# Solving the delta rule's triangular systems in the first stage, pair by pair and group by group

## The chip, the cores and the metric

The kernel runs on one core of a Trainium2 chip. The metric is the device time of one execution in microseconds (us). A core has five engines with instruction queues of their own: TensorE (PE, with its weight loads as PEld), VectorE (DVE), ScalarE (ACT), GpSimd (POOL) and SyncE (SP), which here issues nearly all DMA transfers. Each engine takes its instructions in order; they wait for each other through semaphores. PE multiplies into PSUM banks, and another engine has to copy a bank out before it can be used again.

## The reference

One layer of a hybrid block on 1024 tokens with 16 learned meta tokens ahead of them (L = 1040), 1024 channels, float32:

```python
proj = rms_norm(h) @ w_in                 # attention q, k, v, forget logits; recurrent inputs rw; gates
rw_prev = rw shifted by one token
z = rw + mu * (rw_prev - rw)              # r, k, v and the low-rank inputs zw, za, zg
w = w0 + tanh(zw) @ w_up ; a = sigmoid(a0 + za @ a_up) ; g = sigmoid(zg) @ g_up
# recurrent branch, 8 heads of 64:  S_t = S_(t-1) diag(w_t) + (S_(t-1) a_t) b_t^T + v_t k_t^T ; y_t = S_t r_t
o_rwkv = (group_norm(y) + bonus) * g
o_fox  = forgetting attention of 8 heads of 64
merged = sigmoid(gates) * (o_fox @ w_bf, o_rwkv @ w_br)
h = h + merged @ w_o ; out = h + conv_ffn(rms_norm(h))
```

## The kernel before

All large products are exact to about float32: operands are split into a high and a low part of type fp32r, and `mm3` makes three products of each (lines L201, L202, L203; tiles `mm`, `gate`, `dn`, `aux`). Weights come in pieces of 128x512 (`wf`), from which ACT makes `wh` and POOL `wl`.

Stage 0 normalises the input. Stage 1 prepares the recurrent branch, head pair by head pair (four pairs, p = 0 to 3, of 128 channels): three projections (`zk`, `zr`, `zv`, each in three pieces of 346 or 348 columns by `rw_tile`), the low-rank products (`aux`, L304 to L312, into `sw`, `tha`, `g`), a running sum along the tokens (`cs`, L319), its exponentials `ex` and `ei`, the norm of the keys (`ss`, `inv` with Ln and Exp on ACT and a Newton step on DVE), and from these the tiles `ar_t` and `bk_t` of 17 chunks of 64 tokens. All DVE operations of this kind take the 1088 tokens of a pair in one instruction. `prods` multiplies bk and ar of a chunk (L394) and masks the result into `am` (L395), which goes to the array `am_d` in DRAM. `diags` copies the 32x32 diagonal blocks of `am_d` to a second array `a_d` (L404, four DMAs a pair). `bkt` transposes bk (L411) and stores it through `bt` (L414, L415). `bonus` and transposed values are stored as well. The gate projections serve as filler, and the last of their 84 stage-1 steps are emitted behind pair 3.

Stage 2 begins with `forget` (L582), then merges two streams by hand-set costs: the attention, and the recurrent branch. The latter first solves the triangular systems of two chunks at a time (`rw_pre`, b = 0 to 8): their blocks are loaded from `a_d` to 128 lanes (`la`), a unit matrix to `x`, and 31 steps of a multiplication and an addition on DVE (L449 and L451) invert them. The result goes to `t_d` in DRAM and from there into the diagonal blocks of `am`; 16 products of 32x32 a chunk on PE (`rp`, L474 and L478) give the off-diagonal block. `rw_chain` then takes the 17 chunks one behind the other (`ch`). Stage 3 joins the branches, stages 4 and 5 are the output projection and the convolutional feed-forward.

The text of the program does not fix the order on an engine alone: a scheduler with a model of the chip orders the instructions of each engine when the kernel is built. PSUM has three banks for `mm`, two for `aux`, two shared by `am` and `tp`, and one for `gate` in stage 1.

Of the kernel before, what the change touches and what calls it, by code (L numbers as in the profile page):

```python
# [100 lines left out]
def stage0(S, p0):  # L101
    nc, tc = S.nc, S.tc
# [7 lines left out]

    def tiles(*tags):
        r = []
        for t in tags:
            m = 6 if t[1:] in ("r_t", "k_t") else 3
            r.append(p0.tile([P, m, 348], F32, name="xt", tag=t))
        return r, [(i, j) for i, t in enumerate(r) for j in range(t.shape[1])][:KD]

    xs = []
    for c, (t0, t1) in enumerate(CH):
        n = t1 - t0  # L120
        tl, at = tiles(*(("zr", "zv", "sw"), ("tha", "inv", "ex"), ("ar_t", "cs"))[c])
        k = 0
        for t in tl:
            for j in range(0, t.shape[1], 3):
                m = min(3, KD - k)
                nc.sync.dma_start(out=t[:, j:j + m, :n], in_=S.A["xT"][:, k:k + m, t0:t1])
                k += m
                if k == KD:
                    break
        xs.append([tl[i][:, j] for i, j in at])  # L130
# [1066 lines left out]
```

## Time and profile before

| | us |
|---|---|
| median of 3 runs | 2045.58 (2042.92 to 2048.2) |
| the profiled execution's span | 2045.7 |
| PE busy | 1879.8 (92%) |
| DVE busy | 918.6 (45%) |
| ACT busy | 751.7 (37%) |
| POOL busy | 558.8 (27%) |

The span of the profiled execution is the whole program, so its own time is the span. In the profile each instruction has a start and a duration; a group of instructions with one source line and tile has a minimum, median and maximum duration in ns. A table of stretches gives each engine's busy time in the stretch, the number of its records in brackets (a plain float32 matmul leaves two), the clock granted to PE (PEclk, 1.00 is full speed), the share of the DMA engines and GB/s. The matmuls' records overlap, so the cost of one in a row of them is the distance of their starts. A row of the waits reads "engine, line <- what it waited for: us in total, times, the longest".

### The profile page before, as it was taken

To read this page: it belongs to the slowest core of one execution; us is meant where nothing else is said; L and a number is where in the kernel's file an instruction comes from. 1 tells how busy PE (TensorE), PEld (TensorE's weight loads), DVE (VectorE), ACT (ScalarE), POOL (GpSimd) and SP (SyncE) were. 2 spreads that over 40 slices of the span, in tenths; PEclk is the share of its full clock that TensorE was granted. 3 is DMA by queue.
4 is the path that set the end of the run, shared out by engine and by line. 5 is a ranking of instruction groups with operands and counts; after the bars stand their busy time and mean duration, and the time that the engine had idled before them with its cause. 6 is when DMAs were issued, how large, how long until landed. Compare 5 with 4: busy or idle time off the path is not lost.

```text
span 2045.7 us, 32875 instructions
## 1 busy us (share of the span) xinstructions
PE 1879.8 (92%) x12812; PEld 1699.0 (83%) x12812; DVE 918.6 (45%) x2032; ACT 751.7 (37%) x1603; POOL 558.8 (27%) x552
## 2 busy tenths in 40 slices
PE   7996966747899999999899999999999999999999
PEld 6985855646778888888778999899998998999997
DVE  5264534128678642432764545733232332332333
ACT  5542332214333443443665434532232331322321
POOL 6421111103102211311431234533232332332322
PEclk9997979868999899999999999999999999999999
DMA  4233232541334332222223533211111111111112
GB/s 153 79 104 92 93 95 84 163 109 52 87 109 116 105 95 85 83 65 61 73 87 123 146 120 112 79 42 57 47 42 52 41 53 42 42 57 47 42 48 102
DMA packets 154483, 167.95 MB, mean 82 GB/s; under 512 B 47576, under 2 KB 111112, under 8 KB 154328
## 3 DMA queue, kind: packets, MB, share of 16 engines
q1 hardware_dynamic: 154072, 165.79, 27.0%
q8 instruction: 101, 1.65, 0.3%
q14 instruction: 54, 0.44, 0.1%
q0 software_dynamic: 256, 0.07, 0.0%
HBM read 123.39 MB, written 43.53 MB: 82 GB/s over the span
## 4 chain that ended last, share of the span: by engine, by line
PE 78%; DVE 7%; DMA 6%; SPq 4%; ACT 2%; issue 1%; POOL 0%; ACTq 0%; DVEq 0%; POOLq 0%
PE mm L202 14%; PE mm L201 14%; PE mm L203 14%; PE dn L201 4%; PE dn L203 4%; PE dn L202 4%; SPq L404 3%; PE gate L201 3%; PE gate L202 2%; PE gate L203 2%; PE t L780 2%; PE o L794 2%; PE am L394 2%; DVE x L451 1%; DVE xt L449 1%
## 5 line engine op out<-in xcount | busy, mean ns | idle before, releaser
L189 POOL TENSOR_TENSOR wl<-wf,wh 128x512 fp32r<-128x512 f32 (+1 forms) x268 | 352.6, 1319 | 787.3 <-ACT wh L188 738.2
L202 PE MATMUL mm<-x,wh 128*128 128x344 f32 (+1 forms) x1056 | 339.1, 321 | 0.0
L201 PE MATMUL mm<-x,wh 128*128 128x344 f32 (+1 forms) x1056 | 337.6, 320 | 1.1 <-DVE ug L1029 1.0
L203 PE MATMUL mm<-x,wl 128*128 128x344 f32 (+1 forms) x1056 | 337.4, 320 | 1.0 <-POOL wl L189 1.0
L188 ACT CAST wh<-wf 128x512 fp32r<-128x512 f32 (+1 forms) x268 | 163.7, 612 | 352.6 <-PE dn L202 182.4
L201 PE MATMUL mm<-xh,wh 128*128 128x348 f32 (+4 forms) x624 | 211.8, 341 | 3.6 <-ACT xh L169 1.6
L202 PE MATMUL mm<-xl,wh 128*128 128x348 f32 (+4 forms) x624 | 210.2, 337 | 0.7 <-POOL xl L170 0.7
L203 PE MATMUL mm<-xh,wl 128*128 128x348 f32 (+4 forms) x624 | 209.5, 336 | 0.0
L201 PEld LDWEIGHTS mm<-x,wh 128*128 128x128 f32 x1056 | 199.2, 189 | 1.9 <-ACT uv L1027 1.2
L203 PEld LDWEIGHTS mm<-x,wl 128*128 128x128 f32 x1056 | 199.0, 189 | 1.7 <-POOL wl L189 1.5
L202 PEld LDWEIGHTS mm<-x,wh 128*128 128x128 f32 x1056 | 199.3, 189 | 0.4
L201 PE MATMUL gate<-xh,wh 128*128 128x342 f32 x384 | 142.8, 372 | 2.9 <-ACT sg L834 2.9
L1056 DVE TENSOR_TENSOR h<-h,dn 128x512 f32<-128x512 f32 x96 | 66.0, 689 | 169.0 <-PE dn L203 168.4
L203 PE MATMUL dn<-gh,wl 128*128 128x512 f32 x352 | 138.8, 394 | 0.0
L201 PE MATMUL dn<-gh,wh 128*128 128x512 f32 x352 | 138.6, 394 | 0.0
L202 PE MATMUL dn<-gl,wh 128*128 128x512 f32 x352 | 138.6, 394 | 0.0
L201 PEld LDWEIGHTS mm<-xh,wh 128*128 128x128 f32 x624 | 121.9, 196 | 9.1 <-issue 4.1
L202 PEld LDWEIGHTS mm<-xl,wh 128*128 128x128 f32 x624 | 122.0, 196 | 5.9 <-issue 1.5
L202 PE MATMUL gate<-xl,wh 128*128 128x342 f32 x384 | 126.6, 330 | 0.0
L203 PE MATMUL gate<-xh,wl 128*128 128x342 f32 x384 | 126.2, 329 | 0.0
L203 PEld LDWEIGHTS mm<-xh,wl 128*128 128x128 f32 x624 | 121.8, 195 | 3.7 <-issue 1.0
L1028 DVE SCALAR_TENSOR_TENSOR uv<-mm,par,uv 128x342 f32<-128x342 f32 (+1 forms) x66 | 37.8, 573 | 162.4 <-ACT uv L1027 162.4
(313 smaller groups left out, 3704.2 us busy)
## 6 DMA issues: line engine op xcount, KB each, us to landing
wf<-in_w_up_dram SPq DMA_DIRECT2D x88, 256.0 KB
am<-am_d SPq DMA_DIRECT2D x17, 512.0 KB
sg_d<-sg SPq DMA_DIRECT2D x48, 171.0 KB
sg<-sg_d SPq DMA_DIRECT2D x48, 171.0 KB
wf<-in_w_gate_dram SPq DMA_DIRECT2D x32, 256.0 KB
wf<-in_w_out_dram SPq DMA_DIRECT2D x32, 256.0 KB
wf<-in_w_down_dram SPq DMA_DIRECT2D x32, 256.0 KB
wf<-in_w_rw_dram SPq DMA_DIRECT2D x28, 256.0 KB
```

Of the source, the lines that this page charges most:

```text
L188: nc.scalar.copy(out=wh[:, :n], in_=wf[:, :n])
L189: nc.gpsimd.tensor_tensor(out=wl[:, :n], in0=wf[:, :n], in1=wh[:, :n], op=ALU.subtract)
L201: nc.tensor.matmul(ps, lhsT=wh, rhs=xh, start=first and k == 0, stop=False)
L202: nc.tensor.matmul(ps, lhsT=wh, rhs=xl, start=False, stop=False)
L203: ins = nc.tensor.matmul(ps, lhsT=wl, rhs=xh, start=False, stop=last and k == n - 1)
L394: nc.tensor.matmul(ps[:, j * P:(j + 1) * P], lhsT=bk_t[r, c0 + j, :], rhs=ar_t[r, c0 + j, :], start=True, stop=True)
L404: nc.sync.dma_start(out=S.a_d[:, k, h], in_=S.am_d[:, r, h, r])
L449: nc.vector.tensor_tensor(out=tv, in0=x[:, :ni, s:s + 1].broadcast_to([P, ni, m]), in1=la[:, s:s + 1, s + 1:s + 1 + m].broadcast_to([P, ni ...
L780: S.last_pe = nc.tensor.transpose(ps[:r, (2 * j + e) * 116:(2 * j + e) * 116 + nq], pb[e][i][:nq, k:k + r], S.ident[:nq, :nq])
L794: S.last_pe = nc.tensor.matmul(po[64 * e:64 * e + 64, :nq], lhsT=vt[:r, kb, 64 * e:64 * e + 64], rhs=pt[:r, 2 * j + e, :nq], start=kb == 0 ...
L1028: nc.vector.scalar_tensor_tensor(out=t[:, :n], in0=ps[:, 1:1 + n], scalar=cw(1), in1=t[:, :n], op0=ALU.mult, op1=ALU.add)
L1056: nc.vector.tensor_tensor(out=hs, in0=hs, in1=ps[:], op=ALU.add)
```

## The change

Stage 1 now goes by pair and group of tokens (`G`: 384, 384 and 272 tokens). What was a tile of 1088 tokens is a small tile of 390 columns, all of them drawn from one pool of 28 places (`U`, tag "u"); `ar` and `bk` have six chunks and two places each. The low-rank products take their operands unsplit, one float32 product each in place of three. After the three units of a pair, `solve` inverts that pair's systems on chip: POOL copies the upper left 64x64 of each `am` to `at`; 64 products with the unit matrix bring the 32x32 blocks of 34 chunk-heads and two diagonal places to 98 lanes (`x`); 60 DVE operations invert them; 64 products bring them back, and 64 more make the off-diagonal blocks; one DMA stores `at` as `t_d[p]`. Gone are `a_d`, `la`, the loads of `x` and the stores and loads of `t_d` by parts, and the whole of `rw_pre`. In stage 2 `rw_am` loads `am` and the inverse `tt` for each chunk, and the chain starts at once.

```diff
-CH = [(0, 346), (346, 692), (692, 1040)]
+G = [(0, 384), (384, 768), (768, 1040)]
+NU = 28
...
+def solve(S, p1, p, at):
+    nc = S.nc
+    n = 2 * NCH
+    x = p1.tile([P, 32, 32], F32, name="x", bufs=1)
+    nc.gpsimd.memset(x[32:64], 0.0)
+    for f in range(2):
+        ps = psum(S, "am")
+        for t in range(16):
+            for k in range(2):
+                nc.tensor.matmul(ps[64 * k:64 * k + n, 32 * t:32 * t + 32], lhsT=at[:, :, 32 * k + 16 * f + t],
+                                 rhs=S.ident[0:64, 32 * k:32 * k + 32], start=True, stop=True)
+        for k in range(2):
+            r = slice(64 * k, 64 * k + n)
+            nc.scalar.copy(out=x[r, :, 16 * f:16 * f + 16], in_=ps[r].rearrange("p (t s) -> p s t", s=32))
+    nl = 64 + n
+    nc.gpsimd.memset(x[:nl].rearrange("p s t -> p (s t)")[:, 0:1024:33], 1.0)
+    tmp = p1.tile([P, 240], F32, name="xm", bufs=1)
+    for s in range(1, 31):
+        m = 31 - s
+        tv = tmp[:nl, :s * m].rearrange("p (i t) -> p i t", i=s)
+        nc.vector.tensor_tensor(out=tv, in0=x[:nl, :s, s:s + 1].broadcast_to([nl, s, m]),
+                                in1=x[:nl, s:s + 1, s + 1:].broadcast_to([nl, s, m]), op=ALU.mult)
+        nc.vector.tensor_tensor(out=x[:nl, :s, s + 1:], in0=x[:nl, :s, s + 1:], in1=tv, op=ALU.add)
+    for i, (t0, nt) in enumerate(((0, 11), (11, 11), (22, 10))):
+        ps = psum(S, "am")
+        for t in range(nt):
+            for k in range(2):
+                nc.tensor.matmul(ps[32 * k:32 * k + 32, n * t:n * t + n], lhsT=x[:nl, :, t0 + t],
+                                 rhs=S.ident[:nl, 64 * k:64 * k + n], start=True, stop=True)
+        for k in range(2):
+            r = slice(32 * k, 32 * k + 32)
+            cp = nc.scalar.copy if (i + k) % 2 else nc.vector.tensor_copy
+            cp(out=at[r, :, 32 * k + t0:32 * k + t0 + nt], in_=ps[r, :n * nt].rearrange("p (t c) -> p c t", c=n))
+    hs = p1.tile([64, n, 32], F32, name="hs", bufs=1)
+    nc.vector.transpose(out=hs[0:32], in_=at[0:32, :, 0:32])
+    for f in range(2):
+        ps = psum(S, "am")
+        pv = ps.rearrange("p (h t) -> p h t", t=32)
+        for j in range(16):
+            nc.tensor.matmul(pv[32:64, j], lhsT=at[0:32, 16 * f + j, 32:64], rhs=hs[0:32, 16 * f + j], start=True, stop=True,
+                             tile_position=(0, 32))
+        nc.scalar.copy(out=hs[32:64, 16 * f:16 * f + 16], in_=pv[32:64])
+    for f in range(2):
+        ps = psum(S, "am")
+        pv = ps.rearrange("p (h t) -> p h t", t=32)
+        for j in range(16):
+            nc.tensor.matmul(pv[0:32, j], lhsT=hs[32:64, 16 * f + j], rhs=at[32:64, 16 * f + j, 32:64], start=True, stop=True,
+                             tile_position=(32, 0))
+        nc.scalar.copy(out=at[0:32, 16 * f:16 * f + 16, 32:64], in_=pv[0:32])
+    nc.sync.dma_start(out=S.t_d[p], in_=at[:])
...
+        U = lambda name: p1.tile([P, 390], F32, name=name, tag="u", bufs=NU)
...
+        def proj(p, i):
+            w = wload(S, S.A["w_rw"][2 + 3 * p + i], KD)
+            z = []
+            for c, (t0, t1) in enumerate(G):
+                z.append(U(("zk", "zr", "zv")[i]))
+                rw_tile(S, p1, 2 + 3 * p + i, z[c][:, :t1 - t0], w, c)
+            pads(z[2])
+            return z
...
+        def lora(p, c):
+            pc = slice(p * P, (p + 1) * P)
+            t0, t1 = G[c]
+            n = t1 - t0
+            sw, tha = U("sw"), U("tha")
+            ps = psum(S, "aux")
+            nc.tensor.matmul(ps[:, :n], lhsT=lup[0:64, pc], rhs=wa[0:64, t0:t1], start=True, stop=True)
+            with tc.issue_after(S.last_exp.ins) if p else nullcontext():
+                nc.scalar.activation(out=sw[:, :n], in_=ps[:, :n], func=AF.Tanh, scale=0.5, bias=S.w0h[:, p:p + 1])
+            ps = psum(S, "aux")
+            nc.tensor.matmul(ps[:, :n], lhsT=lup[64:128, pc], rhs=wa[64:128, t0:t1], start=True, stop=True)
+            with tc.issue_after(S.last_exp.ins) if p else nullcontext():
+                S.th = nc.scalar.activation(out=tha[:, :n], in_=ps[:, :n], func=AF.Tanh, scale=0.5, bias=S.a0h[:, p:p + 1])
+            ps = psum(S, "aux")
+            nc.tensor.matmul(ps[:, :n], lhsT=gup[:, pc], rhs=sg[:, t0:t1], start=True, stop=True)
+            g = U("g")
+            nc.scalar.copy(out=g[:, :n], in_=ps[:, :n])
+            nc.sync.dma_start(out=S.g_d[p, :, t0:t1], in_=g[:, :n])
+            nc.gpsimd.tensor_scalar(out=sw[:, :n], in0=sw[:, :n], scalar1=0.5, scalar2=0.5, op0=ALU.mult, op1=ALU.add)
+            if c == 2:
+                pads(sw, tha)
+            return sw, tha
+        def unit(p, c, zk, zr, zv, sw, tha, at):
+            pc = slice(p * P, (p + 1) * P)
+            t0, t1 = G[c]
+            n = t1 - t0
+            nch = -(-n // 64)
+            N = 64 * nch
+            c0 = t0 // 64
+            cs = U("cs")
+            nc.vector.tensor_tensor_scan(out=cs[:, :N], data0=mask[:, :N], data1=sw[:, :N], initial=0.0, op0=ALU.mult, op1=ALU.add)
...
+            ar = p1.tile([P, 6, P], F32, name="ar", bufs=2)
+            bk = p1.tile([P, 6, P], F32, name="bk", bufs=2)
...
+            for b0 in range(0, nch, 3):
+                nb = min(3, nch - b0)
+                am = p1.tile([P, 3, 2, P], F32, name="am", bufs=2)
+                for e in range(2):
+                    r = slice(64 * e, 64 * e + 64)
+                    ps = psum(S, "am")
+                    for j in range(nb):
+                        nc.tensor.matmul(ps[:, j * P:(j + 1) * P], lhsT=bk[r, b0 + j, :], rhs=ar[r, b0 + j, :], start=True, stop=True)
+                    nc.vector.tensor_tensor(out=am[:, :nb, e], in0=ps[:, :nb * P].rearrange("p (c t) -> p c t", t=P),
+                                            in1=S.cmask[:].unsqueeze(1).broadcast_to([P, nb, P]), op=ALU.mult)
+                cc = c0 + b0
+                nc.gpsimd.tensor_copy(out=at[:, 2 * cc:2 * (cc + nb)].rearrange("p (c e) t -> p c e t", e=2), in_=am[0:64, :nb, :, 0:64])
+                nc.sync.dma_start(out=S.am_d[cc:cc + nb, :, 2 * p:2 * p + 2, :].rearrange("c s h t -> s c (h t)"),
+                                  in_=am[:, :nb].rearrange("p c h t -> p c (h t)"))
+            for b0 in range(0, nch, 3):
+                ps = psum(S, "tp")
+                nb = min(3, nch - b0)
+                for j in range(nb):
+                    nc.tensor.transpose(ps[:, j * P:(j + 1) * P], bk[:, b0 + j, :], S.ident[:])
+                bt = U("bt")
+                nc.scalar.copy(out=bt[:, :nb * P], in_=ps[:, :nb * P])
+                nc.sync.dma_start(out=S.bkt_d[c0 + b0:c0 + b0 + nb, :, pc].rearrange("c s k -> s c k"),
+                                  in_=bt[:, :nb * P].rearrange("p (b t) -> p b t", t=P))
...
+            zk = proj(p, 0) if p else zk0
+            zr = proj(p, 1)
+            lo = [lora(p, c) for c in range(3)]
+            with tc.issue_after(S.th.ins):
+                S.ld = nc.scalar.preload_act_table_set("natural_log_exp_and_others")
+            zv = proj(p, 2)
+            at = p1.tile([64, 2 * NCH, 64], F32, name="at", bufs=2)
+            for c in range(3):
+                unit(p, c, zk[c], zr[c], zv[c], *lo[c], at)
+            solve(S, p1, p, at)
...
-            def diags():
-                for k in range(2):
-                    r = slice(32 * k, 32 * k + 32)
-                    for h in (2 * p, 2 * p + 1):
-                        nc.sync.dma_start(out=S.a_d[:, k, h], in_=S.am_d[:, r, h, r])
...
-def rw_load(S, b):
...
-def rw_pre(S, b):
...
+def rw_am(S, c):
+    am = S.rp.tile([P, 8, P], F32, name="am", bufs=2)
+    S.nc.sync.dma_start(out=am[:], in_=S.am_d[c])
+    tt = S.rp.tile([64, 8, 64], F32, name="tt", bufs=2)
+    S.nc.sync.dma_start(out=tt[:].rearrange("s (p e) t -> s p (e t)", p=4),
+                        in_=S.t_d[:, :, 2 * c:2 * c + 2, :].rearrange("p s e t -> s p (e t)"))
+    return am, tt
 def rw_chain(S, c):
-    am = S.rw.pop(c)
-        S.uv, S.bkt = rw_uv(S, 0), rw_bkt(S, 0)
-    (uv, ar), bkt = S.uv, S.bkt
+        S.am, S.uv, S.bkt = rw_am(S, 0), rw_uv(S, 0), rw_bkt(S, 0)
+    (am, tt), (uv, ar), bkt = S.am, S.uv, S.bkt
     if c < NCH - 1:
-        S.uv = rw_uv(S, c + 1)
+        S.am, S.uv = rw_am(S, c + 1), rw_uv(S, c + 1)
...
-        S.last_pe = nc.tensor.matmul(pu[:, h], lhsT=am[0:64, h, 0:64], rhs=pt[:, h, :], start=True, stop=True)
+        S.last_pe = nc.tensor.matmul(pu[:, h], lhsT=tt[:, h, :], rhs=pt[:, h, :], start=True, stop=True)
...
-            def pre():
-                for b in range(9):
-                    yield from rw_pre(S, b)
-            def chain():
-                for c in range(NCH):
-                    while c not in S.rw:
-                        yield 0.5
-                    yield from rw_chain(S, c)
-            yield from merge_streams([(0.0, 1.0, pre()), (50.0, 1.0, chain())])
+            for c in range(NCH):
+                yield from rw_chain(S, c)
...
-        S.a_d = dp.tile([NCH, 2, 8, 32, 32], F32, name="a_d")
-        S.t_d = dp.tile([NCH + 1, 2, 8, 32, 32], F32, name="t_d")
+        S.t_d = dp.tile([4, 64, 2 * NCH, 64], F32, name="t_d")
```

The order on the engines changes at three places. First PE at the end of pair 0, before. `am` and `mm` are the products named above, and the `mm` here are projections of the next pair.

```order
L203 MATMUL mm<-xh,wl 128x348
L201 MATMUL mm<-xh,wh 128x348
L394 MATMUL am<-ar_t,bk_t 128x128 x4
L201 MATMUL aux<-wah,luh 128x346
L202 MATMUL aux<-wal,luh 128x346
L203 MATMUL aux<-wah,lul 128x346
L202 MATMUL mm<-xl,wh 128x348
```

Behind the am group PE has projections and low-rank products of the next pair.

PE at the same place now, from the last projection that stands ahead of the pair's units to the first behind them (`rk` and `kk` are the norm and bonus sums, `at` is the first product of `solve`):

```order
L198 MATMUL mm<-xh,wl 128x274
L424 MATMUL am<-ar,bk 128x128 x12
L435 MATMUL tp<-ident,bk 128x128 x6
L451 MATMUL tp<-ident,zv 128x128 x3
L443 MATMUL aux<-rk,bo 128x384
L396 MATMUL aux<-kk,bo 128x384
L424 MATMUL am<-ar,bk 128x128 x12
...
L396 MATMUL aux<-kk,bo 128x272
L353 MATMUL aux<-wa,lup 128x384
L424 MATMUL am<-ar,bk 128x128 x10
...
L264 MATMUL am<-ident,at 34x32 x64
L196 MATMUL mm<-xh,wh 128x386
```

The three units' small products follow each other with no projection between them.

On DVE the operations of one unit stand in this order now (pair 1, first unit; the same row follows for the second and third):

```order
L379 SCALAR_TENSOR_TENSOR cs<-smask,sw 128x384
L382 TENSOR_TENSOR kf<-kf,zk 128x384
L408 TENSOR_TENSOR bk<-kf,ei 128x6x64
L400 TENSOR_SCALAR ss<-aux 128x384
L611 TENSOR_TENSOR tn<-inv 128x384
...
L614 TENSOR_TENSOR inv<-inv,tn 128x384
L410 SCALAR_TENSOR_TENSOR kk<-zk,par,inv 128x384
L411 SCALAR_TENSOR_TENSOR ar<-kk,ex 128x6x64
...
L415 SCALAR_TENSOR_TENSOR bk<-kk,ei 128x6x64
L425 TENSOR_TENSOR am<-am,cmask 128x3x128 x4
L441 SCALAR_TENSOR_TENSOR rk<-zr,par,kf 128x384
```

Each of them takes what one or two before it made, and the am products stand at the end.

PE at the border of stages 1 and 2, before (`gate` is the filler, `wfh` the forget product):

```order
L394 MATMUL am<-ar_t,bk_t 128x128 x5
L201 MATMUL gate<-xh,wh 128x342
L202 MATMUL gate<-xl,wh 128x342
L203 MATMUL gate<-xh,wl 128x342
L394 MATMUL am<-ar_t,bk_t 128x128
L582 MATMUL mm<-xh,wfh 40x348
```

And now, with the four rows of products of the last `solve`:

```order
L443 MATMUL aux<-rk,bo 128x272
L264 MATMUL am<-ident,at 34x32 x64
L282 MATMUL am<-ident,x 32x34 x64
L294 MATMUL am<-hs,at 32x32 x32
L301 MATMUL am<-at,hs 32x32 x32
L577 MATMUL mm<-xh,wfh 40x348
```

The filler is ahead of them, and the forget products come after the last.

More of the change, by code (lines that the diff above doesn't have):

```diff
@@ L109, in stage0 @@
         nc.gpsimd.memset(S.xl[k][:, 0:2].bitcast(F32), 0.0)
[L111 to L116, printed above, removed]
+    U = lambda name: p0.tile([P, 390], F32, name=name, tag="u", bufs=NU)
     xs = []
-    for c, (t0, t1) in enumerate(CH):
+    for c, (t0, t1) in enumerate(G):
         n = t1 - t0
[L121 to L130, printed above, removed]
         if c == 0:
+            tl = [p0.tile([P, 2, 384], F32, name="xt", tag=("ar", "bk")[k % 2], bufs=2) for k in range(4)]
+            for k in range(4):
+                nc.sync.dma_start(out=tl[k][:, :, :n], in_=S.A["xT"][:, 2 * k:2 * k + 2, t0:t1])
+            xs.append([tl[k // 2][:, k % 2] for k in range(KD)])
             constants(S)
+        else:
+            tl = [U("xt") for _ in range(KD)]
+            for k in range(KD):
+                nc.sync.dma_start(out=tl[k][:, :n], in_=S.A["xT"][:, k, t0:t1])
+            xs.append(tl)
         S.w0.append(wload(S, S.A["w_rw"][c], KD) if c < 2 else wload(S, S.A["w_rw"][c], KD, S.gp, "g", 1, 2))
@@ L136, in stats @@
     def stats(c):
-        n = CH[c][1] - CH[c][0]
+        n = G[c][1] - G[c][0]
         xt = xs[c]
-        tl, at = tiles("bk_t", "kk")
-        sq = [tl[i][:, j, :n] for i, j in at]
+        sq = []
         na = 2
@@ L161, in stage0 @@
     pss = [stats(0)]
-    for c, (t0, t1) in enumerate(CH):
+    for c, (t0, t1) in enumerate(G):
         ps = pss[c]
@@ L277, in stage1, with pads @@
-        z = zs[1]
-        nc.scalar.activation(out=z[0:64, :L], in_=z[0:64, :L], func=AF.Tanh)
-        wah, wal = split(S, p1, z[:, :L], "wa", [P, L])
-        lup, gup = [S.wp.tile([P, 512], F32, name=n, tag="wf", bufs=3) for n in ("lup", "gup")]
+        sg = p1.tile([P, L], F32, name="sgt")
+        wa = p1.tile([P, L], F32, name="wa")
+        zk0 = []
+        def pads(*tiles):
+            for t in tiles:
+                nc.gpsimd.memset(t[:, 272:320], 0.0)
+        for c in stage0(S, p1):
+            t0, t1 = G[c]
+            rw_tile(S, p1, 0, sg[:, t0:t1], S.w0[0], c)
+            nc.scalar.activation(out=sg[:, t0:t1], in_=sg[:, t0:t1], func=AF.Tanh, scale=0.5)
+            nc.gpsimd.tensor_scalar(out=sg[:, t0:t1], in0=sg[:, t0:t1], scalar1=0.5, scalar2=0.5, op0=ALU.mult, op1=ALU.add)
+            rw_tile(S, p1, 1, wa[:, t0:t1], S.w0[1], c)
+            nc.scalar.activation(out=wa[0:64, t0:t1], in_=wa[0:64, t0:t1], func=AF.Tanh)
+            zk0.append(U("zk"))
+            rw_tile(S, p1, 2, zk0[c][:, :t1 - t0], S.w0[2], c)
@@ L881, in stage2 @@
     tc.keep_in_program_order(nc.scalar.preload_act_table_set("natural_log_exp_and_others"))
-    S.rw, S.xla = {}, {}
     S.z = None
@@ L1169, in layout @@
     o["w_down"] = mt(g["ffn_down"][0])
-    xi = np.zeros((4, 32, 8, 32), np.float32)
-    for j in range(4):
-        for c in range(8):
-            xi[j, :, c, 4 * c + j] = 1
-    o["xi"] = xi.reshape(P, 8, 32)
     return o
```

278 lines of the change are left out of this document (74 added, 204 removed).

## The prediction

> **What bounds the kernel now.** I read the page's head first, then PE's busy time by stage, then the holes in it and what ended them, and last the rows of the operations that the change moves.
>
> ```profile
> span 2045.7 us, 32875 instructions
> PE 1879.8 (92%) x12812; PEld 1699.0 (83%) x12812; DVE 918.6 (45%) x2032; ACT 751.7 (37%) x1603; POOL 558.8 (27%) x552
> ```
>
> PE is busy for 92% of the span, so only its 166 idle us and its slow clock can be won, and any PE work that is added counts. The next table cuts the span at marks of the kernel: the first forget matmul (401.0, its row stands first), the first and the last solve operation (445.1, 703.8, rows further down), and 1104, about where stage 3 begins.
>
> ```profile
> L582 PE MATMUL mm<-xh,wfh x24: 318/322/352, 401.0 to 408.5; 128*40 128x348 f32 x16, 128*40 128x344 f32 x8
> ...
> core 0: us, PE busy (x) PEld busy (x) DVE busy (x) ACT busy (x) POOL busy (x), PEclk, DMA share, GB/s
> 0.00:401.00 401.00, 321.95 (x1870) 287.23 (x1870) 166.73 (x258) 149.06 (x269) 112.72 (x142) 0.90 0.35 109
> 401.00:445.00 44.00, 16.27 (x95) 13.67 (x95) 0.52 (x1) 4.55 (x9) 6.33 (x13) 0.71 0.37 81
> 445.00:704.00 259.00, 227.87 (x2013) 196.01 (x2014) 204.21 (x727) 100.13 (x251) 50.35 (x51) 0.91 0.35 93
> 704.00:1104.00 400.00, 385.83 (x3488) 325.84 (x3487) 176.29 (x416) 190.35 (x485) 91.99 (x92) 0.98 0.27 79
> 1104.00:2045.70 941.70, 927.87 (x5350) 876.21 (x5348) 370.84 (x630) 307.60 (x590) 297.38 (x255) 1.00 0.22 69
> ```
>
> Columns are the stretch, each engine's busy us with its records, and the granted clock. Stage 1 (row one) has 79.0 us of PE idle, the start of stage 2 (rows two and three) 58.9 us. The last row has hardly any, and the change does not touch it. In stretches of 50 us the holes are seen better, and five rows of 5 us show one of them and a short one of stage 2:
>
> ```profile
> 0.00:50.00 50.00, 35.58 (x188) 33.99 (x189) 26.90 (x53) 28.75 (x65) 34.97 (x70) 0.93 0.46 156
> 150.00:200.00 50.00, 30.55 (x175) 25.81 (x174) 21.88 (x35) 13.50 (x23) 9.42 (x10) 0.81 0.26 70
> 250.00:300.00 50.00, 31.64 (x172) 27.79 (x172) 16.11 (x17) 14.83 (x26) 7.41 (x9) 0.80 0.32 87
> 350.00:400.00 50.00, 31.79 (x201) 29.14 (x201) 5.44 (x9) 8.84 (x18) 2.12 (x3) 0.75 0.51 151
> ...
> 180.00:185.00 5.00, 0.00 (x0) 0.00 (x0) 0.00 (x0) 0.00 (x0) 0.00 (x0) 0.56 0.10 11
> 200.00:205.00 5.00, 4.78 (x14) 4.03 (x15) 0.49 (x1) 2.33 (x6) 0.00 (x0) 0.50 0.92 269
> 205.00:210.00 5.00, 5.00 (x21) 4.24 (x21) 0.00 (x0) 1.17 (x3) 0.00 (x0) 0.71 0.19 57
> ...
> 520.00:525.00 5.00, 0.60 (x14) 0.38 (x13) 0.87 (x3) 0.34 (x1) 0.00 (x0) 1.00 0.24 48
> 525.00:530.00 5.00, 5.00 (x40) 3.71 (x38) 3.12 (x14) 2.08 (x7) 0.00 (x0) 0.53 0.51 159
> ```
>
> From 180 to about 198 us no engine works, and after it PE runs some 7 us at clock 0.50. The timeline of SP's queue and the waits name the cause:
>
> ```profile
> 168.62 19.16 SPq L404 DMA_DIRECT2D a_d<-am_d  x4
> 187.82 6.87 SPq L415 DMA_DIRECT2D bkt_d<-bt  x2
> ...
> ACT bt L414 <- DMA bkt_d<-bt: 75.6, 8, 23.3
> PE t L657 <- ACT v L653: 29.7, 1, 29.7
> ```
>
> SP stands 19 us in the four a_d copies of a pair; behind them waits the store that frees bt, for which ACT and then PE wait (23.3 us at the longest). The 29.7 us wait in the last row is the hole between 417 and 447, behind pair 3's copies.
>
> **Stage 1: what goes.** Of the 79.0 idle us, 14.4 lie in the first 50, where inputs load; 64.6 can go. Busy time times clock, over seventy 5-us rows from 50 to 400, is 273.5 of 285.8 us, so the slow clock cost 12. All of it at most: -77.
>
> **Stage 1: PE work added.**
>
> ```profile
> core 0: us, PE busy (x) PEld busy (x) ACT busy (x), PEclk, DMA share, GB/s
> 480.00:900.00 420.00, 24.35 (x512) 20.57 (x512) 11.58 (x32) 0.95 0.33 90
> ...
> 657.47 0.69 PE L474 MATMUL rp<-hs,am 32*32 32x32 f32 x16
> ...
> 105.31 1.41 PE L353 MATMUL aux<-kk,bo 128*128 128x346 f32 x4
> 106.42 0.45 PE L201 MATMUL mm<-xh,wh 128*128 128x348 f32 x1
> ...
> 50.00:100.00 50.00, 50.00 (x312) 48.01 (x311) 13.06 (x16) 26.12 (x41) 25.71 (x19) 1.00 0.22 71
> ```
>
> The first row is the rp tile alone, 256 small float32 products in 512 records: 0.095 us each. The second is eight of them at full clock, 0.69 us with the last one's drain of about 0.07: 0.078 each. The solves issue 128 gathers and scatters and 64 block products per pair, 768 in all: 768 x 0.078 = 60 us. These shapes (34x32, 32x34) are not in the trace; below lies 0.05 (the engine overlapping more), 38 us, above 0.095, 73 us; I take 60, since the 32x32 row is the nearest. The lora products become 36 plain float32 ones instead of 108 split ones: the split ones run at 50/312 = 0.16 us, 17 us; two plain float32 products of 346 columns (four records) take from 105.31 to 106.42, 0.555 each, so 0.61 at 384 columns, 22 us: +5. Tiles of 384 and 272 columns instead of 346, with their longer padding and more small operations, I put at 3. Sum +68.
>
> **Stage 1: the unit phases.** A unit is one pair by one token group. Its DVE operations form one chain, from the scan to the am products, and DVE's order runs the three units of a pair one behind the other. PE's order has no projection between the units of pairs 0 to 2: the next pair's zk products stand ahead of unit 1's, and after them PE meets only am, tp and aux of the units. Unit 1's chain is hidden by those zk products (72 of 0.16 us, 11.6); units 2 and 3 are not.
>
> ```profile
> L319 DVE TENSOR_TENSOR_SCAN cs<-smask,sw x4: 2416/2426/3489, 91.0 to 297.7; 128x1088 f32<-128x1088 bf16 x4
> L322 DVE TENSOR_TENSOR kf<-kf,zk x4: 1269/1638/2131, 93.4 to 300.3; 128x1088 f32<-128x1088 f32 x4
> L363 DVE SCALAR_TENSOR_TENSOR ar_t<-kk,ex x4: 2257/2783/3300, 120.0 to 331.9; 128x1088 f32<-128x1088 f32 x4
> L616 DVE TENSOR_TENSOR tn<-inv x12: 501/520/521, 108.8 to 322.0; 128x346 f32<-128x346 f32 x8, 128x348 f32<-128x348 f32 x4
> L358 ACT ACTIVATE inv<-ss x12: 487/494/498, 107.7 to 320.7; 128x346 f32<-128x346 f32 x8, 128x348 f32<-128x348 f32 x4
> L395 DVE TENSOR_TENSOR am<-am,cmask x64: 280/424/692, 128.5 to 400.6; 128x256 f32<-128x256 f32 x48, 128x128 f32<-128x128 f32 x8, 128x512 f32<-128x512 f32 x8
> ```
>
> Scaled to 384 columns: scan 0.9, ar 0.9, kf and four products like it at 0.55 (2.7), ss and four Newton steps like tn, one of them shorter (2.6); Ln and Exp on ACT between them 1.1; four am evictions 0.55 each; rk and bon 1.1: 0.9 + 0.9 + 2.7 + 2.6 + 1.1 + 2.2 + 1.1 = 11.5 us, and with the medians above the minima (POOL beside DVE) 12.4. PE has 12 am, 9 tp and 2 aux products in it, 3.5 us, so it idles 8.5 to 9 us a unit. After each such hole it runs at clock 0.5, as from 200 to 205. Per pair: two holes 17, the tail after unit 3 until the gather 3, and 4 for the slow clock on the units' own products make 24; with the first 7 us of the following products at half clock after each hole, 35. Bounds 14 (unit 1's cover reaches into unit 2) and 35; I take 31, nearer the upper since the row from 180 shows the clock down within 5 us. Three pairs: +93. Pair 3's units have 276 gate products between them, and cost nothing; if that cover is gone, another 20.
>
> The Trainium skill ("TensorE: Matmul & The Clock Gate", Part 1: The HAM clock gate, and HAM oscillation) says that one idle window of about 3.4 us brings the clock to half, and that a kernel whose bursts are short against its waits pays this every time. It speaks against this change: by it every unit starts cold, the 35 of the range. The row 180 to 185 (mean 0.56) agrees.
>
> **Stage 1: the solves.**
>
> ```profile
> L472 DVE STREAM_TRANSPOSE hs<-am x16: 425/432/435, 488.0 to 886.5; 32x256 f32<-32x256 f32 x16
> L480 ACT COPY am<-rp x16: 344/362/367, 494.3 to 891.4; 32x256 f32<-32x256 f32 x16
> ```
>
> Solves of pairs 0 to 2 have projections between their steps in PE's order, and on DVE the evictions of mm stand between the steps; hidden. Per pair DVE does 60 operations of 165 elements on average; from the am row (256 elements 0.42, 512 0.69) 0.155 + 165 x 0.00105 = 0.33, so 20 us a pair. Behind them on DVE waits zv's eviction, and PE behind its bank; that is part of the 31. The last solve has nothing between: gathers 5, four copies of 0.4 us (ACT's 256-column copy and the transposes are in the rows above), DVE 20, scatters 5 and copies 2, a transpose of 1088 columns 1.4, 64 block products 5 and four copies of 0.4 us: 42 us, of which 15 are PE work counted above. Range 20 to 37; with its slow clock at the low end, 30. SP's new t_d store waits for the solve, and behind it stand ar_d and weight loads; those run three tiles ahead, so nothing. POOL gets 24 gather copies of about half a us, off the path.
>
> Stage 1: -77 + 68 + 93 + 30 = +114; forget would start at about 515.
>
> **Stage 2: what goes.** The hole 417 to 447 (idle 27.7), the 31.1 idle us up to 704, the slow clock there (busy times clock is 210.7 of 228.9 in fifty-two 5-us rows, 18), and rp's 20 (its slow part is in the 18).
>
> ```profile
> L449 DVE TENSOR_TENSOR xt<-x,la x263: 157/211/2051, 445.1 to 703.6; 128x60 f32<-128x60 f32 x12, 128x54 f32<-128x54 f32 x8, 128x66 f32<-128x66 f32 x8, 128x28 f32<-128x28 f32 x8
> L451 DVE TENSOR_TENSOR x<-x,xt x263: 124/211/1295, 445.3 to 703.8; 128x60 f32<-128x60 f32 x12, 128x54 f32<-128x54 f32 x8, 128x66 f32<-128x66 f32 x8, 128x28 f32<-128x28 f32 x8
> ```
>
> These 526 operations fill DVE (204 of 259 us busy), and attention's evictions queue behind them; with them gone, a second hole source is late chain steps. In all 97 at most; at stage 2's end (rows 704 to 1104, 14 idle) attention stands alone for longer, since gates and chain end earlier. I keep 17 back for that: -80. Of SP's DMAs there, 88 for la, x and t_d go and 17 tt loads come, one a chunk, two chunks ahead; nothing.
>
> **Sum.** +114 - 80 = +34 on a span of 2045.7; the median of three runs is 2045.58, the same. Forecast 2080.
>
> **The rivals.**
> Faster: the holes stay short. Then the clock does not fall, a pair costs 14: -77 + 68 + 42 + 25 - 80 = -22, 2024; with the cheap gathers (38) 2002. For it: the units' DVE chain is 11.5 us by minima, and after the 4.4 us hole of the row from 520 only some 5 us ran slow. It decides below 19 us a pair.
> No change: 19 to 21 a pair, 2040 to 2052.
> Slower still: half clock throughout. A pair costs 35 (105), gathers at 0.095 (73), the last solve 37, and stage 2 returns only 65: -77 + 81 + 105 + 37 - 65 = +81, 2127. The Trainium skill's rule above ("TensorE: Matmul & The Clock Gate", Part 1: The HAM clock gate), with bursts always shorter than the window, would end here. For it: DVE rows reach 2051 ns where the median is 211, in 263 operations, so DVE steps are stretched at times. Against it: such outliers are few.
> The change not doing what it says (the SP wait stays): the store t_d<-at holds SP as a_d did, 6 us a copy; four copies, 25 more, 2105. It moves 64 rows of 2176 elements, a_d's copies runs of 32; unlikely, and part of the slower cases.
>
> **How the numbers follow.** A measurement here tells about 0.3% (6 us) from no change. Forecast (2052 to 2105) 0.5, slower still 0.15, faster 0.24, same 0.11. So slower 0.65, same 0.11, faster 0.24. The range reaches down to most of the faster case and up to most of the slowest: 2008 to 2118; the forecast's own is 2055 to 2105.
>
> **What would show it.** Right: no a_d rows on SP, no hole after 417 of the old kind; PE holes of 8 to 9 us between am groups, two a pair in pairs 0 to 2, each followed by clock 0.5; one hole of some 28 us split by short bursts before forget, which starts near 515; stage 2 (forget to the first br products) about 80 us shorter. Wrong: units' holes under 5 us, or clock 1.00 through them; the first forget matmul before 480; gather products at other than 0.08 us.

## The result, and the profile after

The changed kernel takes 2076.62 us in the median of four runs (2075.26 to 2079.23), the kernel before 2046.89 (2042.92 to 2051.02): 1.0142 times as long, with a 95% interval of 1.012 to 1.0163. The forecast was 2080, slower.

The head of the page of the changed kernel, its first forget product, and its stages by the same marks as before (forget at 515.3, stage 3 about 1139):

```profile
span 2077.4 us, 34698 instructions
PE 1944.7 (94%) x13800; PEld 1735.0 (84%) x13800; DVE 901.8 (43%) x1797; ACT 774.1 (37%) x1658; POOL 563.7 (27%) x614
...
L577 PE MATMUL mm<-xh,wfh x24: 318/322/513, 515.3 to 524.0; 128*40 128x348 f32 x16, 128*40 128x344 f32 x8
...
core 0: us, PE busy (x) PEld busy (x) DVE busy (x) ACT busy (x) POOL busy (x), PEclk, DMA share, GB/s
0.00:515.30 515.30, 419.82 (x3370) 348.30 (x3370) 267.95 (x565) 180.66 (x356) 118.41 (x204) 0.85 0.28 88
515.30:1139.00 623.70, 598.42 (x5094) 510.79 (x5094) 265.24 (x606) 290.35 (x720) 149.40 (x157) 0.98 0.30 87
1139.00:2077.40 938.40, 926.47 (x5336) 875.92 (x5336) 368.65 (x627) 303.08 (x583) 295.90 (x253) 1.00 0.22 68
```

Stage 1 ends 114.3 us later than before (515.3 against 401.0). From the first forget product to the end it was 2045.7 - 401.0 = 1644.7 us and is now 2077.4 - 515.3 = 1562.1: 82.6 less. So the change loses 114 in one stage and wins 83 in the other. The last rows, from near the start of stage 3, differ by 3 us (941.7 and 938.4).

In stage 1 PE is busier and slower. Rows of 5 us of pair 1's unit phase, then of the last solve, and the waits of PE from 50 to 515:

```profile
225.00:230.00 5.00, 0.91 (x2) 0.30 (x2) 3.24 (x6) 2.74 (x6) 1.06 (x2) 0.81 0.51 159
230.00:235.00 5.00, 0.20 (x1) 0.23 (x2) 4.28 (x8) 0.00 (x0) 0.00 (x0) 0.50 0.12 36
235.00:240.00 5.00, 4.88 (x27) 4.21 (x28) 2.33 (x5) 0.00 (x0) 0.54 (x2) 0.50 0.37 121
...
480.00:515.00 35.00, 18.46 (x290) 14.15 (x286) 22.71 (x64) 4.86 (x10) 0.15 (x1) 0.51 0.01 2
...
PE am L424 <- DVE bk L415: 37.4, 7, 8.1
PE am L282 <- DVE x L277: 11.8, 26, 1.0
```

The am products wait for bk, an operation late in a unit's DVE chain, up to 8.1 us a time. In the last solve PE is busy for 18 us of 35, at half clock. Over 93 rows of 5 us from 50 to 515, idle time is 75.5 us and busy time times (1 - clock), called slow clock below, 45.7; from 50 to 400 before it was 64.2 and 12.4. On SP nothing like the a_d copies is left: the four t_d stores take under half a us each.

```profile
L304 SPq DMA_DIRECT2D t_d<-at x4: 445/452/457, 212.9 to 515.3; - x4
```

### The profile page after: what moved, and what is told of

Same layout as the page of the kernel before. It is cut to its first block, busy times and chain, and to the rows that moved or that the text cites. A ratio compares the mean times of both kernels' runs of the same rounds, so it can differ in the third digit from the quotient of the medians.

```text
span 2077.4 us, 34698 instructions
## 1 busy us (share of the span) xinstructions
PE 1944.7 (94%) x13800; PEld 1735.0 (84%) x13800; DVE 901.8 (43%) x1797; ACT 774.1 (37%) x1658; POOL 563.7 (27%) x614
## 4 chain that ended last, share of the span: by engine, by line
PE 86%; DVE 7%; ACT 3%; DMA 2%; issue 1%; POOL 0%; SPq 0%; DVEq 0%; ACTq 0%; POOLq 0%
PE mm L196 15%; PE mm L198 15%; PE mm L197 15%; PE dn L196 4%; PE dn L198 4%; PE dn L197 4%; PE gate L196 3%; PE gate L197 3%; PE gate L198 3%; PE t L775 2%; PE o L789 2%; PE am L424 2%; PE s L740 1%; PE am L282 1%; PE s L741 1%
## 5 line engine op out<-in xcount | busy, mean ns | idle before, releaser
L184 POOL TENSOR_TENSOR wl<-wf,wh 128x512 fp32r<-128x512 f32 (+1 forms) x268 | 346.6, 1295 | 794.4 <-ACT wh L183 767.5
L196 PE MATMUL mm<-xh,wh 128*128 128x386 f32 (+5 forms) x624 | 211.2, 340 | 2.7 <-ACT xh L164 1.3
L198 PE MATMUL mm<-xh,wl 128*128 128x386 f32 (+5 forms) x624 | 210.2, 337 | 0.0
L197 PE MATMUL mm<-xl,wh 128*128 128x386 f32 (+5 forms) x624 | 209.4, 336 | 0.0
L1041 DVE TENSOR_TENSOR h<-h,dn 128x512 f32<-128x512 f32 x96 | 66.1, 689 | 168.9 <-PE dn L198 168.4
```

Of the source, the lines that this page charges most:

```text
L184: nc.gpsimd.tensor_tensor(out=wl[:, :n], in0=wf[:, :n], in1=wh[:, :n], op=ALU.subtract)
L196: nc.tensor.matmul(ps, lhsT=wh, rhs=xh, start=first and k == 0, stop=False)
L197: nc.tensor.matmul(ps, lhsT=wh, rhs=xl, start=False, stop=False)
L198: ins = nc.tensor.matmul(ps, lhsT=wl, rhs=xh, start=False, stop=last and k == n - 1)
L1041: nc.vector.tensor_tensor(out=hs, in0=hs, in1=ps[:], op=ALU.add)
```

## The experiments

Each run was timed against the kernel before on the same chip; its medians there were 2048.91 beside runs 1 to 4, 2052.15 beside runs 5 to 8 and 2049.52 beside runs 9 to 12. "Idle" and "slow clock" are sums over 5-us rows, as above, from 50 to the first forget product where nothing else is said.

**1. The solve's inner part left out.** In `solve` all lines between its start and the last DMA are gone.

```diff
 def solve(S, p1, p, at):
     nc = S.nc
     n = 2 * NCH
-    x = p1.tile([P, 32, 32], F32, name="x", bufs=1)
-    ...
     nc.sync.dma_start(out=S.t_d[p], in_=at[:])
```

> The changed kernel without the inner part of solve: the tile at goes to DRAM as it was gathered, so the inverse is missing; all else stays. Theory (solve's own 768 products cost 60 us of PE, and the last solve stands bare for 30 more): about 1987, forget starting near 425. Rival (the products of pairs 0 to 2 lie in holes that are there anyway, since the units' DVE chains set the pace): only the last solve goes, about 2035, forget near 475.

It took 2002.44 us (0.9769 of the kernel before, 0.9754 to 0.9785), 74 less than the changed kernel, and forget starts at 439.9, 75 earlier:

```profile
50.00:439.90 389.90, 323.81 (x1689) 272.99 (x1688) 149.30 (x255) 128.45 (x247) 85.92 (x142) 0.83 0.30 93
```

Neither time came. PE's work (busy time times clock) fell by 64 us, from 343.7 to 279.5, so the products did cost PE time, near the 60 forecast. But idle time fell only from 75.5 to 66.1 and slow clock from 45.7 to 44.4. The holes of stage 1 are there without any solve. The 75 us do not come evenly: from the first scan of a pair to that of the next it takes 90.4, 91.6 and 94.0 us in place of 102.0, 103.0 and 101.9, so the first three solves were worth 31 us together, and from the last pair's first scan to forget it takes 62.8 in place of 107.0, 44 less.

**2. and 6. Projections between the units.** First only zk of the next pair, then zk and zr:

```diff
-            zk = proj(p, 0) if p else zk0
+            zk = zkn if p else zk0
...
             for c in range(3):
                 unit(p, c, zk[c], zr[c], zv[c], *lo[c], at)
+                if wn:
+                    zkn.append(U("zk"))
+                    rw_tile(S, p1, 5 + 3 * p, zkn[c][:, :G[c][1] - G[c][0]], wn, c)
```

> The changed kernel with the three zk pieces of the next pair written one behind each unit instead of after the solve; PE's order then has 24 projections (4 us) in the hole of each unit of pairs 0 to 2. Theory (units leave PE idle and its clock down because nothing stands between their products): 4 of 8.5 us of six holes covered, 24, and 10 to 20 of slow clock: 2035 to 2045. Rival (DVE sets the pace of stage 1, so that PE waits elsewhere instead, in the solve for instance): 2070 to 2080.

> The changed kernel with the zk and zr pieces of the next pair written behind each unit, and zv behind the solve; PE's order has 48 projections (8 us) in each hole of the units, as long as the hole measured (8.0 us). Theory (cover only pays where it fills the hole, so that the clock stays up; with 24 it did not): clock 1.00 in the unit phases, idle 50 to 515 down from 75 to about 45, 2020 to 2045. Rival (cover is only moved: what stands between units is missing in the solves and ahead of unit 1, and the holes open there): 2070 to 2090.

2085.47 us (1.0172, 1.0155 to 1.0189) and 2078.04 us (1.0112, 1.0082 to 1.0142): 9 more than the changed kernel by the medians (its ratio was 1.0142, and the intervals meet), and the same. Both theories fell. Run 6 came in its rival's range, run 2 some 5 us above its own. With zk alone, idle time fell from 75.5 to 64.9 but slow clock rose from 45.7 to 62.6. With zk and zr it was 66.3 and 61.2. The chains on DVE show where the cover was taken from. First the changed kernel, then the run with zk and zr, both with the first unit's scan of pair 0, a first or second operation of its solve, and the first scan of pair 1:

```profile
101.35 0.95 DVE L379 TENSOR_TENSOR_SCAN cs<-smask,sw 128x384 f32<-128x384 bf16 x1
161.80 0.19 DVE L275 TENSOR_TENSOR xm<-x 98x30 f32<-98x30 f32 x1 [3.23 <-ACT x L268]
203.38 1.34 DVE L379 TENSOR_TENSOR_SCAN cs<-smask,sw 128x384 f32<-128x384 bf16 x1
```

```profile
99.53 0.95 DVE L379 TENSOR_TENSOR_SCAN cs<-smask,sw 128x384 f32<-128x384 bf16 x1
163.52 0.19 DVE L275 TENSOR_TENSOR xm<-x 98x30 f32<-98x30 f32 x1 [3.12 <-ACT x L268]
194.26 0.95 DVE L379 TENSOR_TENSOR_SCAN cs<-smask,sw 128x384 f32<-128x384 bf16 x1
```

In the changed kernel a pair takes 102 us: 60.5 from its first scan to its solve, 41.6 from there to the next pair's scan. In the other run the first part is 64.0 and the second 30.7 here; over three pairs (scans at 99.5, 194.3, 299.9, 399.6) the period is 94.8, 105.6 and 99.7, 100 in the mean. What the units gained in cover lengthened them, and the solves had it no more.

The trace also shows why the cover lengthened the units, a rival that neither expectation names: PE takes most of these projections ahead of the unit's own kk product, for which the DVE chain waits. The DVE operation that takes that product, in pair 1's second unit, in the changed kernel, with zk, and with zk and zr:

```profile
228.21 0.55 DVE L400 TENSOR_SCALAR ss<-aux 128x384 f32<-128x384 f32 x1
234.09 0.56 DVE L400 TENSOR_SCALAR ss<-aux 128x384 f32<-128x384 f32 x1 [3.76 <-PE aux L396]
227.61 0.56 DVE L400 TENSOR_SCALAR ss<-aux 128x384 f32<-128x384 f32 x1 [2.37 <-PE aux L396]
```

Behind it PE still idles until bk is made (5.7 us with zk), so its clock falls to 0.50 again for the am products. These runs therefore tried cover in front of a link of the chain; projections behind that link were not tried.

**3. More filler for the last solve.**

```diff
-                fill(S, 84)
+                fill(S, 120)
```

> The changed kernel with 120 instead of 84 filler steps of gates behind stage 1; PE's order has some 117 gate products (19 us) between the products of the last solve, which are missing later in stage 2. Theory (the last solve's 30 us are idle time and slow clock): 20 to 30 less, 2047 to 2057, forget near 512 although 19 us more work stands ahead of it, and the clock at 1.00 in the solve. Rival (stage 2 needs these gates for its own holes): stage 2 gives it back, 2070 to 2080.

2095.15 us (1.0226, 1.0203 to 1.0249), 18 more than the changed kernel. Forget moved from 515.3 to 526.7: 23 us more work stands ahead of it, and only some 13 of idle time and slow clock went. From forget to the end it takes 1563.7 us where the changed kernel takes 1562.1, though that work is no longer to be done there: the products are missing at the end of stage 2. This run, then the changed kernel:

```profile
1100.00:1150.00 50.00, 42.24 (x280) 31.90 (x281) 16.75 (x48) 19.03 (x59) 3.96 (x4) 0.73 0.11 34
```

```profile
1100.00:1150.00 50.00, 45.46 (x318) 40.03 (x317) 18.46 (x47) 24.76 (x67) 7.09 (x7) 0.93 0.36 114
```

The rival's direction came, and more of it than its range (2070 to 2080).

**4. The kernel before with its a_d copies by rows.** The same elements, with another dimension outermost:

```diff
-                        nc.sync.dma_start(out=S.a_d[:, k, h], in_=S.am_d[:, r, h, r])
+                        nc.sync.dma_start(out=S.a_d[:, k, h].rearrange("c s t -> s c t"),
+                                          in_=S.am_d[:, r, h, r].rearrange("c s t -> s c t"))
```

> The kernel before with the a_d copies' dimensions in another order, the 32 rows outermost instead of the 17 chunks; same elements, same runs of 32. Theory (SP's wait of 6 us a copy comes from how the copy is spread over the DMA engines, and makes the holes of stage 1): a copy holds SP under 2.5 us, the holes at 178, 268, 343 and 417 shrink by 10 to 19 us each, 1985 to 2010. Rival (the hold goes with the number of runs, or the holes come from the chain of DVE at the pair's end): hold 6 us and 2040 to 2050, or a short hold and a time within 10 us of before.

1962.76 us: 0.9576 of the kernel before (0.9554 to 0.9598), 86 us less, and the fastest of the runs that compute the whole block.

```profile
L404 SPq DMA_DIRECT2D a_d<-am_d x16: 544/628/1494, 168.4 to 338.4; - x16
...
L582 PE MATMUL mm<-xh,wfh x24: 317/321/327, 333.1 to 340.4; 128*40 128x348 f32 x16, 128*40 128x344 f32 x8
...
180.00:185.00 5.00, 5.00 (x29) 4.13 (x28) 0.94 (x1) 1.42 (x5) 0.00 (x0) 1.00 0.78 225
0.00:333.00 333.00, 311.25 (x1870) 279.03 (x1870) 166.28 (x258) 148.92 (x269) 113.19 (x142) 0.98 0.42 131
```

A copy holds SP for 0.63 us in the median. In the kernel before the sixteen were:

```profile
L404 SPq DMA_DIRECT2D a_d<-am_d x16: 586/6021/6438, 168.6 to 417.4; - x16
```

Forget starts 68 us earlier (333.1), idle time from 50 on falls from 64 to 7 us and the slow clock from 12 to 1. The holes of stage 1 before were SP's wait in these copies, and this line takes them away without any part of the change. The Trainium skill ("DMA: Bandwidth & Descriptors", Why a DMA increments its semaphore by 16 and not by 1) says that the number of DMA engines is the largest count up to 16 that divides the outermost dimension of both sides. By it 17 chunks give one engine and 32 rows give 16. The trace goes the same way: a DMA share of 0.10 and 11 GB/s from 180 to 185 before, 0.78 and 225 GB/s in the row above. It does not count engines: one of 16 would be a share of 0.06, and other transfers run in the second row.

**5. PE kept warm.** Extra products of 128x128 behind the kk product of each unit of pairs 0 to 2, into the bank of the gates:

```diff
-            nc.tensor.matmul(ps[:, :n], lhsT=S.bo[:], rhs=kk[:, :n], start=True, stop=True)
+            mk = nc.tensor.matmul(ps[:, :n], lhsT=S.bo[:], rhs=kk[:, :n], start=True, stop=True)
+            if p < NP_ - 1:
+                wm = psum(S, "gate")
+                for j in range((16, 24, 16)[c]):
+                    with tc.issue_after(mk.ins):
+                        mk = nc.tensor.matmul(wm[:, :128], lhsT=S.bo[:], rhs=S.ident[:], start=True, stop=True)
```

> The changed kernel with 16, 24 and 16 extra products of 128x128 (results unused, a PSUM bank that is free there) behind the kk product of each unit of pairs 0 to 2: some 37 us more PE work at full clock, all of it in holes. Theory (half of what the unit phases cost is not the hole but the slow clock behind it, for the units' own products and the gathers): slow-clock loss in stage 1 falls from 46 to about 20, time 2048 to 2060, though PE does more. Rival (the DVE chain alone sets the units' pace, the slow clock hides in the holes): 2074 to 2085.

2084.21 us (1.0151, 1.0127 to 1.0174): the rival's range. By the ratio this is the changed kernel's time (1.0142). Slow clock fell only to 39, not to the 20 of the theory, and idle time to 49. Pair 0's unit phase, in the changed kernel and in this run:

```profile
110.00:165.00 55.00, 35.57 (x262) 26.95 (x261) 30.79 (x60) 13.34 (x29) 8.75 (x18) 0.60 0.36 111
```

```profile
110.00:165.00 55.00, 46.07 (x384) 38.92 (x383) 30.48 (x66) 14.43 (x30) 8.72 (x18) 0.78 0.35 111
```

The clock rises from 0.60 to 0.78, and DVE does the same in the same time. The gathers start at 154.15 instead of 156.44 there, and 39 us of added work in stage 1 eat more than that: forget starts at 521.2, 6 later.

The run does not show what a full clock would be worth. In the third unit the products still run at half clock, since the extra ones end before bk is made:

```profile
145.00:150.00 5.00, 3.61 (x19) 3.34 (x20) 2.38 (x6) 0.00 (x0) 0.50 (x1) 0.57 0.22 66
150.00:155.00 5.00, 4.43 (x40) 2.77 (x41) 1.86 (x5) 1.28 (x4) 0.68 (x2) 0.50 0.69 220
```

And in pairs 1 and 2 the extra products push back the projections behind which the first unit's am products stand on PE. That unit takes 24.7 and 25.2 us there from scan to scan, where the changed kernel takes 21.9 and 21.5:

```profile
218.38 1.02 DVE L430 TENSOR_TENSOR am<-am,cmask 128x384 f32<-128x384 f32 x2 [5.20 <-PE am L429]
```

Nor is a unit's chain DVE's alone. In the changed kernel DVE itself waits for the units' products (rows of its waits from 50 to 515):

```profile
DVE am L425 <- PE am L424: 47.5, 27, 4.9
DVE bon L445 <- PE aux L443: 33.2, 12, 4.9
```

At half clock these waits are longer. From the first am product to the next scan pair 1's first unit, at full clock, takes 6.5 us (218.8 to 225.2) and its second, at half clock, 8.1 (234.8 to 242.9). So the slow clock costs a unit some 2 us; for the seven such units of pairs 0 to 2 that is an estimate of 12 to 15 us out of the 45.7, and the rest lies beside the chain.

**10. A shorter chain.** The Newton step of the units is left out:

```diff
-            newton_rsqrt(nc, inv[:, :n], ss[:, :n], 0.0, tn[:, :n])
```

> The changed kernel without the Newton step in the units (four DVE operations, 2.0 us of 384 columns; the norm of the keys is less exact). Theory (the DVE chain of a unit sets the length of the unit phase, one us for one): nine units of pairs 0 to 2 shorter by 2.0, pair 3's hidden by gates: 15 to 22 less, 2055 to 2062. Rival (the unit phases are set by PE at half clock and by ACT's part of the chain): 2070 to 2077.

2058.4 us (1.0042, 1.0029 to 1.0055), 18 less than the changed kernel; forget starts at 492.2, 23 earlier. The theory's number came, but not from nine units alike. The four operations take 2.04 us in a unit of 384 columns and 1.6 in one of 272, 5.7 a pair. The 23 us come from other places: 3.5 ahead of the first scan, then 8.6, 3.7 and 2.4 in pairs 0 to 2 (from a pair's first scan to the next pair's), and 4.9 from pair 3's first scan on, where the gates were to hide them. The second units are shorter by 2.4, 2.4 and 1.6, about one for one. The first units of pairs 1 and 2 are as long as before, since their am products stand behind projections on PE, and DVE waits for them instead. In pair 1, the changed kernel, then this run:

```profile
219.75 1.02 DVE L425 TENSOR_TENSOR am<-am,cmask 128x384 f32<-128x384 f32 x2 [2.82 <-PE am L424]
206.71 1.02 DVE L424 TENSOR_TENSOR am<-am,cmask 128x384 f32<-128x384 f32 x2 [4.10 <-PE am L423]
```

So the chain sets the pace where nothing stands ahead of a unit's products on PE. Why the start and pair 0 gained more than the operations cost was not tested.

**9. Projections between the units, and no solve.** Runs 1 and 6 together.

> The run with zk and zr between the units (2078), and the inner part of solve left out as in the first run without it (2002): the inverse is missing. Theory (units and solves are one serial chain on DVE, about 100 us a pair, so that projections put between the units are only missing in the solves; without the solves they cover): 1940 to 1975. Rival (projections between the units bring nothing in any case, since the units' own chain is as long as before): 1995 to 2010.

1987.99 us (0.9704, 0.968 to 0.9728), 14 less than run 1, between the two ranges: without solves, projections between the units do bring something, where with solves they brought nothing; but half of the least that the theory gave (27). They lengthen the units here too, to 34.8 and 36.2 us for the first of pairs 1 and 2 (21.6 and 22.2 in run 1), where DVE now waits up to 16.0 us for ACT's kf operation, behind the pair's low-rank products.

**8. and 11. Stage 2's return.** Both start from run 4, whose stage 2 has 80 us of idle time and slow clock (47.7 and 32.3, from 330 to 1015) where the changed kernel has 34 (from 515 to 1130).

```diff
-        ni, m = s // 4 + 1, smax - s
+        ni, m = 1, 1
```

> The same kernel (a_d copies by rows) with every solve step cut to one column: the same 526 DVE operations, each about 0.16 instead of 0.26 us, and the inverse is not computed. Theory (stage 2's return of 80 us in the changed kernel is mostly DVE's time in the solves): DVE's 50 us less bring 20 to 35 us, 1928 to 1943. Rival (what is late is the way of the inverse through DRAM and the chain's start): 1955 to 1963.

```diff
+        if s % 3 and s != 2:
+            yield 0.5
+            continue
         ni, m = s // 4 + 1, smax - s
```

> The kernel before with a_d copies by rows (1963) and 12 of the 31 solve steps of each system, so some 206 of 526 DVE operations; the inverse is not right. Theory (DVE's queue full of solve steps makes the idle and slow 80 us of stage 2): DVE's 80 us less bring 25 to 45 us, 1918 to 1938. Rival (the way of the inverse through DRAM and the chain's late start make them): 1950 to 1963.

1957.09 us (0.9536, 0.9505 to 0.9567) and 1945.96 us (0.949, 0.9473 to 0.9507). The small steps bring 6 us, in the rival's range and within what the two intervals leave open; DVE's busy time from 333 to 600 fell only from 194 to 174 us, since a step of one column still takes 0.16 us. A third of the steps (204 DVE operations) brings 17, between the two ranges:

```profile
333.00:600.00 267.00, 239.34 (x2127) 208.04 (x2125) 131.79 (x405) 104.33 (x260) 56.82 (x65) 0.92 0.39 105
```

DVE is down to 132 us, and idle time and slow clock of stage 2 to 65 (from 330 to 1000). So fewer solve steps bring 17 us of the 46 between run 4 and the changed kernel. They also end sooner (the last starts at 474.6 instead of 614.7), so that DVE's time and the chain's earlier start are not told apart. Whether the other 29 are the remaining steps or the way of the inverse through DRAM stays open.

**7. and 12. Spreading the solves of run 4.** A planner's cost of 0.7 for a solve step, then 0.6 and less filler behind stage 1:

```diff
-        yield 0.5
+        yield 0.7
```

> The kernel before with its a_d copies by rows (the run that took 1963) and a cost of 0.7 instead of 0.5 for a solve step in the planner of stage 2, so that the systems are spread over more of the attention. Theory (80 us of idle and slow clock are left in stage 2 because DVE is full of solve steps in its first 270 us): 1935 to 1955. Rival (the chain then ends later than the attention, and the end of stage 2 opens): 1963 or more.

```diff
-        yield 0.5
+        yield 0.6
...
-                fill(S, 84)
+                fill(S, 66)
```

> The kernel before with a_d copies by rows, a cost of 0.6 for a solve step and 66 instead of 84 filler steps behind stage 1, so that 9 us of gates are left for the end of stage 2, where the run with 0.7 lost 41 us. If the front gains half of the 20 us that 0.7 brought and the end is covered: 1945 to 1958. If the end still opens: 1965 to 1980.

1983.17 us (0.9658, 0.9635 to 0.9681) and 1966.92 us (0.9596, 0.9574 to 0.9619). The first came as its rival said: up to 950 it has 18 us less idle time and slow clock than run 4 (60 against 78), and from there to 1050 some 40 more. The second is no faster than run 4, in the range for an end that still opens. Run 4, one line, beats both kernels by 86 and 114 us.

## Why the prediction was right

The forecast was 2080 and +34 on the span; the span rose by 31.7. Its steps:

- *Old stalls of stage 1, -77.* Run 4 removes their cause alone and moves forget by 68. The other 9 are not SP's wait.
- *Work added, +68.* Work before forget rose by 64 us (306.5 to 370.8), and leaving the solves out took 64 away. So the solves' products are all of it, and the 5 for the low-rank products and the 3 for the column groups do not show. The products were put at 0.078 us each, 60; 64 over 768 is 0.084. By kind they are unlike: 64 gathers back to back take 4.1 us, 0.064 each, while the scatters, which PE takes two at a time, are 35.9 us of busy time for 256, 0.140 each. So a sign that was to show the forecast wrong, gathers at other than 0.08, came without harm to the sum. No row shows the 0.07 us for the drain of the last product, on which the 0.078 rests.
- *Unit phases, +93.* Run 1, which has the units and no solve, starts forget 107 us after run 4, which has the pair-wide tiles and no SP wait. PE's work before forget is the same in both (306.9 and 307.2), so the 107 are idle time and slow clock, 14 more than forecast.
- *Last solve, +30.* The 35 us from 480 hold 16.5 us of idle time and about 9 of slow clock, 26. But leaving out all solves gave back only 75 where 60 + 30 were reckoned: 44 at the last solve, put at 42 in all, and 31 in the other three, where 45 of products were reckoned. In part those three fill time that the units' structure leaves idle otherwise.
- *Stage 2, -80.* Measured 82.6. Of the SP hole there I reckoned 27.7; run 4 shortens the time from forget to the end by 18 (1644.7 to 1626.7). Fewer solve steps on DVE are shown to bring 17 us.

In one row, by the starts of forget in run 4, run 1 and the changed kernel: stage 1 lost 68, gained 107 and gained 75, where the forecast had 77, 101 (93 + 5 + 3) and 90 (60 + 30). So the mechanism came, and the sum is better than its terms: the old stalls and the solves were each put too high, the units too low, and that these cancel to within a microsecond of the +114 is luck.

The holes came nearly as forecast: 8.0 us in the second units and, in the third, 2.0 and 3.4 where 8.5 to 9 was said. In pair 1:

```profile
234.80 4.50 PE L424 MATMUL am<-ar,bk 64*128 64x128 f32 x24 [8.07 <-DVE bk L415]
...
246.02 1.65 PE L353 MATMUL aux<-wa,lup 64*128 64x384 f32 x2 [2.03 <-DVE ss L400]
251.05 4.08 PE L424 MATMUL am<-ar,bk 64*128 64x128 f32 x20 [3.38 <-DVE bk L415]
```

But a unit is longer than the 12.4 us that its chain was put at. The second unit takes 17.7 from scan to scan, and 5.0 of that are DVE's waits for the unit's own products, which run at half clock (1.8, 1.1 and 2.1). The forecast had PE's products only inside the chain's time, where they are links of it.

One reason in it stays unproven. The 35 a pair of the upper bound, from which the 31 was taken, charged the products behind each hole at half clock as time of their own. The size fits (19 us idle and 15 of slow clock in pair 0 from 110 to 165). Of that, the units' own products cost some 2 us a unit; for the rest runs 5 and 10 give no price, since run 5 kept the clock up in part of the units only. By the rule of the Trainium skill's page "TensorE: Matmul & The Clock Gate" (HAM oscillation) the clock falls in such holes, and the trace agrees (0.50 in the row from 230).

Of the rivals, "the holes stay short" fell with the holes of 8 us. The t_d store as a new SP wait fell with 0.45 us a store.

## What to carry to other kernels

Before work is moved away from a stalled queue, look at the instruction that stalls it: here the order of a copy's dimensions was worth 86 us, and rebuilding the stage around it cost 30. Filler that is moved from one hole to another gains nothing if the place it leaves opens as wide, and it lengthens the chain if PE takes it ahead of a product for which the chain waits: look where in the order of the engine it lands. Where a serial chain paces a stretch, shortening it helps (18 us here), and more PE work beside it did not.

## What the runs showed that I had not expected

- A DRAM-to-DRAM copy of 17x32x32 elements holds its issuing queue 6.02 us in the median with the 17 outermost, and 0.63 us with the 32 rows outermost.
- Projections worth 4 us put between the units raised the slow-clock loss from 46 to 63 us, more than the 11 that they took from the idle time: PE took most of them ahead of the unit's kk product.
- The same units without any solve had nearly as much idle time and slow clock (110 us) as with the solves (121 us).
